# Splitting four weight pieces during the first slabs, loading the memory tokens later, and moving the softmax scaling ahead of the next scores in the third mixer

## Chip, cores and metric

The kernel runs on one core of a Trainium2 chip. The metric is the device time of one execution in microseconds (us), as the median over several runs; lower is better. The profile is of one execution, with its own time.

## The reference

There are 256 tokens of width 1024, in fp32. Two layers of a first block are followed by one layer of a second.

```
# first_block, for each of 2 layers
x = LN(alpha*x + 0.5*swiglu(x, gate[l,0], up[l,0], down[l,0]))      # first FFN
mem_kv = mem @ w_kv_mem[l]                                        # 256 memory tokens
u = x @ w_in
tok = short_conv_mixer(u) if l == 0 else mlstm_mixer(u)
xa = memory_cross_attention(u[..., -256:], mem_kv)
x = LN(alpha*x + concat(tok, xa) @ w_out[l])
x = LN(alpha*x + 0.5*swiglu(x, gate[l,1], up[l,1], down[l,1]))
# second_block
h = LN(x);  proj = h @ w_in
gates = sigmoid(g_logits + b_gate)                                # 3 branches of 1024
merged = gates[0]*y_pool + gates[1]*y_conv + gates[2]*y_mla       # "third mixer"
h = LN(alpha2*h + merged @ w_out)
h = LN(alpha2*h + moe(h) + ple(p, h))                             # top 2 of 16 experts
```

y_mla is attention of 8 heads with 96-wide queries and keys over two blocks of 128 queries: scores, a mask by chunks of 64, softmax, times the values. y_conv holds a causal depthwise convolution of 31 taps.

## The kernel before

**Arithmetic.** Each fp32 operand is split in a high part (a cast to fp32r) and a low part (the rest), and each product is three matmuls: high by high, low by high, high by low.

**The weight stream.** The weights of the first block and of the third mixer are one list of pieces of 128 x 1024. SyncE loads blocks of two pieces (the first blocks hold one or two) into three raw buffers (`load`, L284). `cast` (L297) writes the high part `wh` of a piece on ScalarE, and `low` (L305) the low part `wl` on VectorE; both go to one of 10 slots of a ring, whose numbers are in the names (`wh4`, `wl4`). A slot is free when `release` has been called for the piece that held it. `st.pump(n)` splits up to n further pieces at that place in the program if slots are free. The load of the block two ahead is issued when the first piece of a block is cast. Every engine works through its instructions in the order in which the program issues them.

**The start.** `first` calls `start_slabs`, which multiplies the pieces 0 to 3 (gate and up weights of the first 256 hidden columns) with the two token tiles, called slabs 0 and 1, while the input is still being transposed. `evacA(t, ps)` then takes the silu on ScalarE (`fs`, L435) and the product with the up part on VectorE (`fm`, L437). Next, `mem_load` issues three loads on ScalarE's queue: `par`, a table of small parameters, and the two tiles of `mem` (L715, L718). After it, `body` of the FFN runs: `slabT(t)` transposes a slab's hidden values on TensorE (L444) and splits them (`fhh` on ScalarE, L583); `gu(f, 0, T)` multiplies the gate and up pieces of hidden block f (pieces 4 and 5 for f=2, 6 and 7 for f=3); `both(f)` multiplies with the down pieces. `mem_T` transposes the memory tokens from f=3 on (L688).

**The third mixer.** `merge(0, ...)` multiplies gate pieces (`g`, `G`) and branch pieces (`y`) in the order of `MERGE_PLAN[0]`, and after each takes one step (one word) of the generator `mla()`, whose order is the string `MLA_PLAN` (L151). s, n, t and o stand for scores, norm, turn and out, and the digit for one of four chains (two blocks of queries by two halves of the heads). `scores` has matmuls (L1566) and then, for each of two groups of heads, a mask, a row maximum and its scaling on VectorE (L1571, L1573, L1574), and two exponentials on ScalarE (L1577). `norm` has a reciprocal on VectorE (L1584) and four scalings on ScalarE (L1587). `turn` transposes the probabilities on TensorE (L1599) and copies them on ScalarE; `out` multiplies with the values (L1613). Between them `merge` also pumps the stream and runs steps of the convolution: `tap` issues three taps on VectorE (L1654), `tap3` a group on TensorE (L1646) with diagonals that ScalarE writes (L1642). The gate's product `gb` is L1731.

Of the kernel before, what the change touches and what calls it, by code (L numbers as in the profile page):

```python
# [147 lines left out]
OFF_Q = 1536  # L148
OFF_GATE = 2208
MERGE = (0, 2, 1)  # L150
MLA_PLAN = "s0 s1+n0 - t0+n1 - o0+t1 - o1+s2 s3+n2 - t2+n3 - o2+t3 o3"  # L151
TAPS_BODY = "1110"
TAPS_POOL = "1011112312111112", "0000010111010111"
TAPS_MLA = "1111111010202032", "1111111010000000"
# [239 lines left out]
class FFN:  # L394
# [59 lines left out]
    def body(self):  # L454
        st = self.st
        self.acc = [[self.k.acc() for _ in range(2)] for _ in range(2)]

        def both(f):
            for t in range(2):
                self.down(f, t, t == 1)  # L460
            st.pump(2)

        self.slabT(0)
        st.pump(2)
        self.gu(2, 0, T)
        self.slabT(1)
        st.pump(2)
        for f in range(3, NF):
            self.gu(f, 0, T)
            st.pump(2)  # L470
            if f == 3:
                both(0)
                both(1)
            if f == 8:
                self.k.load_gb(self.nc.gpsimd if self.k.lnrow else self.nc.scalar)
            if f <= NF - self.last:
                both(f - 1)
            if self.li == (0, 0):
                if 0 < KV_AT[0] - f <= 2:
                    self.k.mem_T(f - KV_AT[0] + 2)  # L480
                if f in KV_AT:
                    self.k.memkv(*divmod(KV_AT.index(f), 3))
        for f in range(NF - self.last, NF):
            self.down(f, 0, False)
            st.pump(2)
        return self.acc
# [13 lines left out]
class Kernel:  # L500
# [17 lines left out]
    def mm(self):  # L518
        self.cmm = (self.cmm + 1) % self.nmm
        return self.slot(self.cmm)  # L520
# [65 lines left out]
    def mm3(self, out, lh, ll, rh, rl, first, last):  # L586
        mm = self.nc.tensor.matmul
        mm(out, lh, rh, start=first, stop=False)  # L588
        mm(out, lh, rl, start=False, stop=False)  # L589
        mm(out, ll, rh, start=False, stop=last)  # L590
# [599 lines left out]
    def start_slabs(self, f):  # L1190
        nc, st = self.nc, self.st
        mm = nc.tensor.matmul
        keys = [("gu", 0, 0, j) for j in range(4)]
        self.warmup = self.ringp.tile([P, P], F32, name=f"wh{RING - 1}")
        nc.vector.memset(self.warmup, 0.0)
        self.wps = self.mm()
        self.warm(8)
        tr = [self.transpose_steps(self.X[t], t, self.xh, self.xl) for t in range(2)]
        next(tr[0])
        self.warm(3)  # L1200
        ps = [self.mm() for _ in range(2)]
        hl = {}

        def part(t, js, x, late=False):
            s = slice(t * P, (t + 1) * P)
            for j in js:
                w = hl[j][x]
                for k in range(2):
                    kk = 2 * j + k
                    mm(ps[t], (self.xl if late else self.xh)[:, kk, s], w[:, k * 512:(k + 1) * 512],  # L1210
                       start=x + late + kk == 0, stop=x == 1 and kk == KT - 1)

        def get(j):
            st.cast()
            st.low()
            hl[j] = st.hl[j]

        get(0)
        get(1)
        part(0, (0, 1), 0)  # L1220
        for _ in tr[0]:
            pass
        part(0, (0, 1), 1)
        next(tr[1])
        get(2)
        get(3)
        for x in range(2):
            part(1, (0, 1), x)
        for _ in tr[1]:
            pass  # L1230
        part(0, (2,), 0)
        part(1, (2,), 0)
        part(0, (2,), 1)
        part(1, (2,), 1)
        part(0, (3,), 0)
        part(1, (3,), 0)
        part(0, range(4), 0, True)
        part(0, (3,), 1)
        f.evacA(0, ps[0])
        part(1, range(4), 0, True)  # L1240
        part(1, (3,), 1)
        for key in keys:
            st.release(key)
        f.evacA(1, ps[1])

    def first(self):
        fs, ws, fe = 0.5 / ALPHA, 1.0 / ALPHA, EPS / ALPHA ** 2
        f = FFN(self, 0, 0, "right")
        self.start_slabs(f)
        self.mem_load()  # L1250
        acc = f.body()
        self.slab_eng, self.slab_pumps, self.slab_ahead = self.nc.vector, 3, 2
        self.conv_open()
        self.ln_boundary(acc, fs, fe, f.tail, self.conv_head)
        acc = self.conv_body()
        g = FFN(self, 0, 1, "right")
        self.ln_boundary(acc, ws, fe, self.wout_tail, g.head)
        acc = g.body()
        f = FFN(self, 1, 0, "left")
        self.ln_boundary(acc, fs, fe, g.tail, f.head)  # L1260
        acc = f.body()
        self.ml_open()
        self.ln_boundary(acc, fs, fe, f.tail, self.ml_head)
        acc = self.ml_body()
        g = FFN(self, 1, 1, "right", LAST2)
        self.ln_boundary(acc, ws, fe, self.wout_tail, g.head)
        acc = g.body()
        return g, acc, fs, fe
# [280 lines left out]
    def mla(self):  # L1549
# [71 lines left out]

        for w in MLA_PLAN.split():
            if w != "-":
# [332 lines left out]
    def routing(self, p, mid):  # L1956
# [26 lines left out]

        gk = new("gk", 4)
        first(gs, misc[:, 148:152], 4, gk)
        ts(gk, gk, -1.0, 1e30, op0=OP.add, op1=OP.mult)
        sv = sel.rearrange("p t (g e) -> p t g e", g=4)
# [464 lines left out]
```

## Time and profile before

| | before |
|---|---|
| median of 3 runs | 1568.85 us (1566.15 to 1569.3) |
| profiled execution: its own time | 1567.56 us |
| profiled execution: span | 1565.6 us |
| mean granted TensorE clock | 0.989 |
| TensorE busy | 1515.4 us (97%) |
| VectorE busy | 881.5 us (56%) |
| ScalarE busy | 654.0 us (42%) |

The span is what the profiler records from the first instruction to the last, and the profiled execution's own time lies 1.96 us above it. A busy share is the time of an engine's own instructions over the span. The granted clock is a share of 2.4 GHz, so 0.50 is 1.2 GHz. PE is TensorE, DVE is VectorE, ACT is ScalarE, POOL is GpSimd, SP is SyncE.

### The profile page before, as it was taken

The page shows a single profiled execution, that of the slowest core. Times are in us where ns is not written, and L with a number is a line of the kernel's source. Part 1 is how long each engine was busy: PE and PEld are TensorE (multiplying, and loading weights), DVE is VectorE, ACT ScalarE, POOL GpSimd, SP SyncE. Part 2 cuts the span into 40 slices and gives each one's busy share as a digit, 9 for nine tenths or more (in the row PEclk, how much of TensorE's full clock was granted, in tenths as well). Part 3 has the DMA queues.
Part 4 walks back from the last instruction along what each step waited for, and adds up shares of the span by engine and source line. Part 5 has one row for each costly group of instructions (what it writes and reads, how often), then busy time and mean ns, then how long its engine had stood idle before and what let it go on. Part 6 is the DMA issues. An engine that isn't in the chain of part 4 may idle for free.

```text
span 1565.6 us, 23697 instructions
## 1 busy us (share of the span) xinstructions
PE 1515.4 (97%) x9725; PEld 1249.0 (80%) x9726; DVE 881.5 (56%) x1399; ACT 654.0 (42%) x1060; POOL 41.9 (3%) x63
## 2 busy tenths in 40 slices
PE   7999999999999999999999999989989999999996
PEld 6899998989999899998878999968879975434432
DVE  3565457775555755457867555578788565222223
ACT  3454445544444344445653444465654531111111
POOL 0000000000000000001001000020000000000001
PEclk9899999999999999999999999999999999999998
DMA  6465554445555454545334644535426666999991
GB/s 219 171 239 209 188 189 163 164 186 215 184 193 188 180 206 183 188 176 202 125 132 181 231 173 179 189 135 205 153 95 229 221 264 262 415 356 414 418 416 71
DMA packets 55985, 332.98 MB, mean 213 GB/s; under 512 B 6320, under 2 KB 6640, under 8 KB 24384
## 3 DMA queue, kind: packets, MB, share of 16 engines
q1 hardware_dynamic: 53424, 319.68, 54.0%
q0 software_dynamic: 1872, 9.52, 1.8%
q10 hardware_dynamic: 576, 2.22, 0.4%
q8 instruction: 78, 1.28, 0.3%
q14 instruction: 35, 0.29, 0.1%
HBM read 330.34 MB, written 1.05 MB: 212 GB/s over the span
## 4 chain that ended last, share of the span: by engine, by line
PE 81%; DVE 9%; ACT 5%; DMA 2%; issue 2%; POOL 0%; SPq 0%; ACTq 0%; DVEq 0%; POOLq 0%
PE mm L598 12%; PE mm L600 12%; PE mm L599 11%; PE mm L2119 7%; PE acc L589 6%; PE acc L588 6%; PE acc L590 6%; PE mm L2142 4%; DVE wl L305 3%; DMA raw<-in_ws_dram 2%; ACT wh L297 2%; PE acc L598 1%; PE acc L599 1%; PE acc L600 1%; PE mm L2088 1%
## 5 line engine op out<-in xcount | busy, mean ns | idle before, releaser
L305 DVE TENSOR_TENSOR wl<-raw,wh 128x1024 fp32r<-128x1024 f32 (+1 forms) x403 | 474.3, 1217 | 137.1 <-ACT wh L297 136.4
L598 PE MATMUL mm<-xh,wh 128*128 128x256 f32 x1608 | 456.8, 284 | 8.9 <-ACT wh L297 6.8
L297 ACT CAST wh<-raw 128x1024 fp32r<-128x1024 f32 (+1 forms) x404 | 403.0, 1044 | 138.4 <-PE acc L590 45.7
L600 PE MATMUL mm<-xh,wl 128*128 128x256 f32 x1608 | 453.6, 282 | 1.2 <-DVE wl L305 1.2
L599 PE MATMUL mm<-xl,wh 128*128 128x256 f32 x1608 | 453.7, 282 | 0.0
L598 PEld LDWEIGHTS mm<-xh,wh 128*128 128x128 f32 x1608 | 305.8, 190 | 14.9 <-ACT wh L297 7.3
L600 PEld LDWEIGHTS mm<-xh,wl 128*128 128x128 f32 x1608 | 305.8, 190 | 1.7 <-DVE wl L305 1.7
L599 PEld LDWEIGHTS mm<-xl,wh 128*128 128x128 f32 x1608 | 305.3, 190 | 2.1
L414 ACT ACTIVATE fs<-mm 128x256 f32<-128x256 f32 x80 | 30.7, 384 | 293.5 <-PE mm L600 293.3
L416 DVE TENSOR_TENSOR fm<-fs,mm 128x256 f32<-128x256 f32 x80 | 33.6, 421 | 211.7 <-ACT fs L414 211.7
L588 PE MATMUL acc<-wh,fhh 128*128 128x512 f32 x352 | 139.8, 397 | 2.4 <-ACT wh L297 2.4
L589 PE MATMUL acc<-wl,fhh 128*128 128x512 f32 x352 | 140.4, 399 | 0.8 <-DVE wl L305 0.8
L590 PE MATMUL acc<-wh,fhl 128*128 128x512 f32 x352 | 139.7, 397 | 0.0
L588 PEld LDWEIGHTS acc<-wh,fhh 128*128 128x128 f32 x352 | 67.0, 190 | 16.0 <-ACT wh L297 2.6
L590 PEld LDWEIGHTS acc<-wh,fhl 128*128 128x128 f32 x352 | 66.9, 190 | 15.7
L589 PEld LDWEIGHTS acc<-wl,fhh 128*128 128x128 f32 x352 | 66.8, 190 | 14.2 <-DVE wl L305 1.1
L584 DVE TENSOR_TENSOR fhl<-fm,fhh 128x256 fp32r<-128x256 f32 x80 | 34.0, 426 | 37.8 <-ACT fhh L583 37.8
L2123 ACT ACTIVATE es<-mm 128x256 f32<-128x256 f32 x16 | 6.1, 383 | 110.9 <-PE mm L2119 110.9
L583 ACT CAST fhh<-fm 128x256 fp32r<-128x256 f32 x80 | 32.5, 406 | 45.0 <-DVE fm L416 45.0
L651 POOL TENSOR_TENSOR rs_r<-rs_v,nhalf 128x1 f32<-128x1 f32 (+3 forms) x21 | 17.8, 847 | 1198.4 <-DVE rs_v L649 1154.1
L2157 DVE SCALAR_TENSOR_TENSOR X<-mm,ws,X 64x512 fp32r<-64x512 f32 x32 | 24.0, 750 | 37.3 <-ACT X L2154 36.7
L2124 DVE TENSOR_TENSOR es<-es,mm 128x256 f32<-128x256 f32 x16 | 6.7, 421 | 66.2 <-ACT es L2123 66.2
(609 smaller groups left out, 2127.2 us busy)
## 6 DMA issues: line engine op xcount, KB each, us to landing
raw<-in_ws_dram SPq DMA_DIRECT2D x196, 1024.0 KB, 4.9
wh<-in_we_dram SPq DMA_DIRECT2D x56, 512.0 KB, 11.2
wl<-in_we_dram SPq DMA_DIRECT2D x56, 512.0 KB, 11.2
w<-in_we_dram SPq DMA_DIRECT2D x22, 1024.0 KB, 11.3
raw<-in_we_dram SPq DMA_DIRECT2D x18, 1024.0 KB, 11.9
gb<-in_lnp_dram POOLq DMA_DIRECT2D x5, 1024.0 KB, 5.2
w<-in_wg_dram SPq DMA_DIRECT2D x2, 1024.0 KB, 7.7
raw<-in_ws_dram SPq DMA_DIRECT2D x2, 896.0 KB, 4.7
```

The costliest lines, as they stand in the source:

```text
L297: self.nc.scalar.copy(h[:, :n], src)
L305: self.eng.tensor_sub(l, src, h)
L416: nc.vector.tensor_tensor(m[:, :n], s[:, :n], ps[:, n:2 * n], op=OP.mult)
L584: self.nc.vector.tensor_sub(l, src, h)
L588: mm(out, lh, rh, start=first, stop=False)
L589: mm(out, lh, rl, start=False, stop=False)
L590: mm(out, ll, rh, start=False, stop=last)
L598: mm(out, h[:, c], xh[:, k, s], start=k == 0, stop=False)
L599: mm(out, h[:, c], xl[:, k, s], start=False, stop=False)
L600: mm(out, l[:, c], xh[:, k, s], start=False, stop=k == kn - 1)
L2119: nc.tensor.matmul(ps[64 * b:64 * b + 64], x, w[:, c:c + 512], start=d == 0, stop=d == KT - 1)
L2142: self.nc.tensor.matmul((pb if i else pa)[64 * i:64 * i + 64], hT[:, a, 64 * b:64 * b + 64], w[:, c:c + 512], start=k == 0, stop=k == 3)
```

## The change

Three edits. (1) `start_slabs` pumps two pieces when slab 1's input transposes have been issued, and one after each `evacA`: pieces 4 to 7 are split there, not in `body`. (2) `mem_load` is called in `body` of the first FFN, behind `slabT(1)` and the pump after it. (3) `MLA_PLAN` is another string of 14 words with the same 16 operations: each norm stands a word earlier against the scores behind it, and some words are empty.

```
--- before.py
+++ after.py
@@ -148,7 +148,7 @@
 OFF_Q = 1536
 OFF_GATE = 2208
 MERGE = (0, 2, 1)
-MLA_PLAN = "s0 s1+n0 - t0+n1 - o0+t1 - o1+s2 s3+n2 - t2+n3 - o2+t3 o3"
+MLA_PLAN = "s0 - n0+s1 - t0 n1 o0+t1 o1+s2 - n2+s3 - t2+n3 o2+t3 o3"
 TAPS_BODY = "1110"
 TAPS_POOL = "1011112312111112", "0000010111010111"
 TAPS_MLA = "1111111010202032", "1111111010000000"
@@ -465,6 +465,8 @@
         self.gu(2, 0, T)
         self.slabT(1)
         st.pump(2)
+        if self.li == (0, 0):
+            self.k.mem_load()
         for f in range(3, NF):
             self.gu(f, 0, T)
             st.pump(2)
@@ -1228,6 +1230,7 @@
             part(1, (0, 1), x)
         for _ in tr[1]:
             pass
+        st.pump(2)
         part(0, (2,), 0)
         part(1, (2,), 0)
         part(0, (2,), 1)
@@ -1237,17 +1240,18 @@
         part(0, range(4), 0, True)
         part(0, (3,), 1)
         f.evacA(0, ps[0])
+        st.pump(1)
         part(1, range(4), 0, True)
         part(1, (3,), 1)
         for key in keys:
             st.release(key)
         f.evacA(1, ps[1])
+        st.pump(1)
 
     def first(self):
         fs, ws, fe = 0.5 / ALPHA, 1.0 / ALPHA, EPS / ALPHA ** 2
         f = FFN(self, 0, 0, "right")
         self.start_slabs(f)
-        self.mem_load()
         acc = f.body()
         self.slab_eng, self.slab_pumps, self.slab_ahead = self.nc.vector, 3, 2
         self.conv_open()
```

ScalarE at the program's start, from the last cast of the first four pieces on (`raw` are the raw buffers, `mm` PSUM tiles). Before:

```order
L297 CAST wh3_166<-raw_80 128x1024
L435 ACT_TABLE_LOAD
L435 ACTIVATE fs_202<-mm2_126 128x256
L435 ACTIVATE fs_216<-mm3_127 128x256
L715 DMA par_71<-in_par_dram 128x230
L718 DMA mem0_224<-in_mem_dram 128x1024
L718 DMA mem1_225<-in_mem_dram 128x1024
L583 CAST fhh_235<-mm0_232 128x128
L583 CAST fhh_239<-mm0_232 128x128
L297 CAST wh4_245<-raw_132 128x1024
L297 CAST wh5_249<-raw_132 128x1024
L414 ACTIVATE fs_304<-mm1_253 128x256
```

And in the changed kernel, from the same cast on (line numbers of `body` are higher by two there):

```order
L297 CAST wh3_166<-raw_80 128x1024
L297 CAST wh4_182<-raw_132 128x1024
L297 CAST wh5_186<-raw_132 128x1024
L435 ACT_TABLE_LOAD
L435 ACTIVATE fs_212<-mm2_126 128x256
L297 CAST wh6_218<-raw_160 128x1024
L435 ACTIVATE fs_232<-mm3_127 128x256
L297 CAST wh7_236<-raw_160 128x1024
L585 CAST fhh_247<-mm0_244 128x128
L585 CAST fhh_251<-mm0_244 128x128
L297 CAST wh8_257<-raw_180 128x1024
L297 CAST wh9_261<-raw_180 128x1024
```

Two of the four casts now stand ahead of slab 0's silu and one behind each silu; the three loads are gone from here: six rows lie between the last row shown and them, the last two of which are the casts into slots 0 and 1.

VectorE in the third mixer around the first reciprocal (`sm`), from the last reduction of the first scores on. Before:

```order
L1574 TENSOR_SCALAR mx_11076<-mx_11076 128x2
L305 TENSOR_TENSOR wl2_11085<-raw_10937,wh2_11084 128x1024
L1654 SCALAR_TENSOR_TENSOR cz_10432<-cz_10432,par_71 128x256 x3
L1571 MEMSET acc_11116 64x2x64
L1573 TENSOR_REDUCE mx_11124<-acc_11116 128x2
L1574 TENSOR_SCALAR mx_11124<-mx_11124 128x2
L1571 MEMSET acc_11117 64x2x64
L1573 TENSOR_REDUCE mx_11131<-acc_11117 128x2
L1574 TENSOR_SCALAR mx_11131<-mx_11131 128x2
L1584 RECIPROCAL sm_11067<-sm_11067 128x4
L305 TENSOR_TENSOR wl3_11143<-raw_10937,wh3_11142 128x1024
```

And in the changed kernel, where lines of `mla` and `merge` are higher by four:

```order
L1578 TENSOR_SCALAR mx_11076<-mx_11076 128x2
L305 TENSOR_TENSOR wl2_11085<-raw_10937,wh2_11084 128x1024
L1658 SCALAR_TENSOR_TENSOR cz_10432<-cz_10432,par_71 128x256 x3
L305 TENSOR_TENSOR wl3_11117<-raw_10937,wh3_11116 128x1024
L1658 SCALAR_TENSOR_TENSOR cz_10432<-cz_10432,par_71 128x256 x6
L1735 SCALAR_TENSOR_TENSOR gb_10911<-sg_10076,acc_10912 128x256
L1588 RECIPROCAL sm_11067<-sm_11067 128x4
L1575 MEMSET acc_11145 64x2x64
L1577 TENSOR_REDUCE mx_11153<-acc_11145 128x2
L1578 TENSOR_SCALAR mx_11153<-mx_11153 128x2
```

The reciprocal now stands ahead of the second scores' reductions, but behind one more subtraction, six more taps and one gate product, as TensorE's second scores come one gate piece and one branch piece later.

## Rows read from the trace of the kernel before

**Rows 1.** The page's totals, and its chain that ended last, by engine.

```profile
PE 1515.4 (97%) x9725; PEld 1249.0 (80%) x9726; DVE 881.5 (56%) x1399; ACT 654.0 (42%) x1060; POOL 41.9 (3%) x63
...
PE 81%; DVE 9%; ACT 5%; DMA 2%; issue 2%; POOL 0%; SPq 0%; ACTq 0%; DVEq 0%; POOLq 0%
```

**Rows 2.** Windows: length; busy PE, PEld, DVE, ACT, POOL; clock; DMA share; GB/s.

```profile
160.00:560.00 400.00, 397.72 (x2705) 363.90 (x2705) 250.22 (x338) 182.68 (x276) 6.99 (x12) 1.00 0.51 187
560.00:1115.00 555.00, 546.08 (x3576) 487.56 (x3575) 351.07 (x525) 273.49 (x433) 21.35 (x24) 1.00 0.49 177
1320.00:1520.00 200.00, 200.00 (x967) 82.65 (x967) 47.04 (x98) 29.93 (x52) 2.70 (x6) 1.00 1.00 404
```

**Rows 3.** Timeline, TensorE's start: start, us, instruction, [idle before, releaser].

```profile
26.29 0.58 PE L598 MATMUL mm<-xh,wh 128*128 128x256 f32 x1 [3.72 <-ACT wh L297]
...
61.76 0.49 PE L688 MATMUL mm<-ident,mem 128*128 128x128 f32 x3
```

**Rows 4.** Windows of the start, columns as in the windows above.

```profile
22.19:61.76 39.57, 28.38 (x138) 24.59 (x137) 17.18 (x21) 14.38 (x21) 0.00 (x0) 0.78 0.45 164
26.30:32.60 6.30, 5.83 (x25) 5.54 (x26) 2.33 (x2) 0.88 (x1) 0.00 (x0) 0.50 0.66 247
40.20:43.10 2.90, 2.89 (x13) 2.90 (x14) 1.09 (x1) 0.00 (x0) 0.00 (x0) 0.51 0.27 42
49.90:56.70 6.80, 6.04 (x15) 4.66 (x15) 6.50 (x6) 4.38 (x6) 0.00 (x0) 0.50 0.52 196
```

**Rows 5.** Timeline of the start, ScalarE, its queue of DMA issues, and VectorE.

```profile
13.07 2.01 ACT L297 CAST wh<-raw 128x1024 fp32r<-128x1024 f32 x2
15.10 1.28 ACT L435 ACT_TABLE_LOAD   x1
16.45 1.28 DVE L695 TENSOR_TENSOR xl<-acc,xh 128x512 fp32r<-128x512 f32 x2
20.06 0.38 ACT L435 ACTIVATE fs<-mm 128x256 f32<-128x256 f32 x1 [3.68 <-PE mm L1210]
22.80 1.56 ACTq L718 DMA_DIRECT2D mem<-in_mem_dram  x2
25.19 1.99 ACT L297 CAST wh<-raw 128x1024 fp32r<-128x1024 f32 x2
```

**Rows 6.** The raw loads issued at 8 to 12 us: duration, starts, landing.

```profile
L284 SPq DMA_DIRECT2D raw<-in_ws_dram x2: 327/327/327, 9.2 to 10.9; - x2
...
DMA to landing us min/median/max: 7.4/7.7/8.1
```

**Rows 7.** Third mixer: TensorE's waits (sum, times, longest) in 1105 to 1190, and windows.

```profile
PE acc L1599 <- ACT pr L1587: 6.9, 3, 3.1
...
1120.00:1180.00 60.00, 51.23 (x360) 45.51 (x359) 45.51 (x106) 35.81 (x95) 3.18 (x6) 0.94 0.33 121
1130.00:1135.00 5.00, 2.55 (x18) 1.89 (x17) 1.91 (x7) 4.22 (x15) 0.00 (x0) 1.00 0.01 3
1140.00:1145.00 5.00, 4.08 (x11) 2.90 (x12) 3.91 (x9) 4.90 (x14) 0.00 (x0) 0.72 0.00 0
```

**Rows 8.** Timeline of the third mixer, VectorE and TensorE, in order of time.

```profile
1127.38 1.23 DVE L305 TENSOR_TENSOR wl<-raw,wh 128x1024 fp32r<-128x1024 f32 x1 [2.98 <-ACT wh L297]
1128.53 1.27 DVE L1654 SCALAR_TENSOR_TENSOR cz<-cz,par 128x256 f32<-128x256 f32 x3
1132.73 1.20 PE L1599 MATMUL acc<-ident,pr 128*128 128x128 f32 x4 [2.45 <-ACT pr L1587]
1135.66 2.46 DVE L1654 SCALAR_TENSOR_TENSOR cz<-cz,par 128x256 f32<-128x256 f32 x6
1138.04 0.41 DVE L1731 SCALAR_TENSOR_TENSOR gb<-sg,acc 128x256 f32<-128x256 f32 x1
1139.84 0.17 DVE L1584 RECIPROCAL sm<-sm 128x4 f32<-128x4 f32 x1
1140.56 1.21 PE L1599 MATMUL acc<-ident,pr 128*128 128x128 f32 x4 [3.15 <-ACT pr L1587]
```

More of the change, by code (lines that the diff above doesn't have):

```diff
@@ L150 @@
 MERGE = (0, 2, 1)
-MLA_PLAN = "s0 s1+n0 - t0+n1 - o0+t1 - o1+s2 s3+n2 - t2+n3 - o2+t3 o3"
+MLA_PLAN = "s0 - n0+s1 - t0 n1 o0+t1 o1+s2 - n2+s3 - t2+n3 o2+t3 o3"
 TAPS_BODY = "1110"
@@ L467, in body @@
         st.pump(2)
+        if self.li == (0, 0):
+            self.k.mem_load()
         for f in range(3, NF):
@@ L1230, in start_slabs @@
             pass
+        st.pump(2)
         part(0, (2,), 0)
@@ L1239, in start_slabs @@
         f.evacA(0, ps[0])
+        st.pump(1)
         part(1, range(4), 0, True)
@@ L1244, in start_slabs @@
         f.evacA(1, ps[1])
+        st.pump(1)
     def first(self):
@@ L1249, in first @@
         self.start_slabs(f)
-        self.mem_load()
         acc = f.body()
```

## The prediction

> **What bounds the kernel now.** I read the page's totals first: TensorE is busy for 97% of the span, and 81% of the chain that ended last is its own matmuls; VectorE has 9%, ScalarE 5% [rows 1]. So the question is where TensorE does not run, or runs at a lower clock. The windows of the long middle, 160 to 1115 us, have TensorE busy in 397.7 of 400 and 546.1 of 555 us at a granted clock of 1.00, and the window 1320 to 1520 in all of it [rows 2]. Little is to be had there. Two places remain.
>
> The first is the program's start. From the start of slab 0's transposes at 22.19 us to the memory transposes at 61.76 [rows 3] lie 39.57 us, of which TensorE is busy for 28.38 at a mean clock of 0.78 [rows 4]. It waits 3.72 us for the first cast of pieces 4 and 5 [rows 3], and three windows, each behind such a wait, run at a granted 0.50 or 0.51, the 1.2 GHz level: 6.30, 2.90 and 6.80 us [rows 4].
>
> The second is the third mixer's attention: in 1120 to 1180 TensorE stands for 60 − 51.23 = 8.77 us, and its clock is 0.94 [rows 7]. Of this idle time 6.9 us stands ahead of three `turn` transposes, which wait for ScalarE's scaling of the probabilities (largest 3.1) [rows 7]. VectorE is busy for 45.5 of those 60 us [rows 7], so it has only some 14 us to spare there.
>
> **The start, step by step.** No instruction is added or taken away; the splits of pieces 4 to 7 are moved ahead, and the loads of `par` and `mem` behind.
>
> - *Why pieces 4 to 7 are late now.* Their casts are issued behind slab 1's evacuation and behind the issues of the three loads of `mem_load`: ScalarE is issuing from 22.80 on (the two of `mem` alone 1.56 us), and its two casts begin at 25.19 [rows 5]. The raw block of pieces 4 and 5 had been loaded long before: issued at 9.2, 7.4 us to landing, so there at 16.6; that of 6 and 7 issued at 10.9, 8.1 us, so there at 19.0 [rows 6].
> - *Pieces 4 and 5 after.* ScalarE ends the casts of pieces 2 and 3 at 15.1 [rows 5] and waits for the block at 16.6; two casts of 2.01 us together [rows 5] take it to 18.6, and the table load of 1.28 [rows 5], which now stands behind them, to 19.9. Slab 0's silu starts at 20.06 now [rows 5], so it is not delayed, by 0.2 us. VectorE ends the two tiles of `xl` at about 17.7 [rows 5]; two subtractions of 1.23 [rows 8] end at 20.2, before slab 0's product needs it at 20.4. Both pieces are split some 2 us before TensorE wants them at 22.6.
> - *Pieces 6 and 7.* One cast behind slab 0's silu (20.4 to 21.5), one behind slab 1's (22.8 to 23.8); the last subtraction ends near 25.1. Step f=2 of the FFN keeps TensorE until about 28.2, so this is hidden with 3 us to spare.
> - *Later pieces.* Each raw buffer comes free when its subtractions end, so the loads of the next blocks go out about 6 to 9 us earlier than now, as the subtractions do; with 8.1 us each to landing [rows 6], pieces 8 and 9 are there by about 24.7 and wanted at 34, 10 and 11 by 28.2 and wanted at 40.
> - *The memory tokens.* Their issues now stand in ScalarE's queue behind the casts of pieces 10 and 11, by my walk at 33 to 35 us. With the landing time of the raw loads, 8.1 us, as a bound, they are there by 43.1; the transposes want them at about 42.7. That is nothing, or half a microsecond of waiting. The issues take about 2 us of ScalarE at 33 to 35, hidden by the matmuls of f=3. `par` has no reader before the first mixer.
> - *The sum.* In the three half-clock windows TensorE is busy for 5.83 + 2.89 + 6.04 = 14.76 us [rows 4]; at the full clock that is 7.38. The idle part of the whole stretch is 39.57 − 28.38 = 11.19. If no wait is left, the clock stays up and the gain is **18.6 us**. Some of the busy time that is left is pipeline overlap at a slow clock, so I take 19. Lower end 17: half a microsecond for the memory tokens and one short stretch at the lower clock. Upper end 20.
>
> What would stand late next? Nothing in the 1050 us behind: TensorE is the bound there [rows 2], loads go out when the pieces ahead of them are used, and so all of it moves with it. In the last stage TensorE is at 200 of 200 us and DMA at 1.00 [rows 2], but its loads too are issued when a tile comes free. The gain is kept.
>
> **The third mixer.** The first normalisation (`n0`: one reciprocal on VectorE, four scalings on ScalarE) now comes ahead of the second scores `s1`, and some `turn` and `out` steps come earlier. Again nothing is added.
>
> - *turn0.* Now the reciprocal stands behind the reductions of s1, and turn0 starts at 1132.73 after 2.45 us of waiting [rows 8]. In the new order the reciprocal has ahead of it wl2 (from 1127.38), three taps of the convolution, wl3, six taps and a gate: 1128.53 + 1.27 + 1.23 + 2.46 + 0.41 = 1133.9 [rows 8]. From a reciprocal at 1139.84 to its turn at 1140.56 it is 0.72 [rows 8], so turn0 starts at about **1134.6**, later than now. TensorE has in the meantime one more y (12 matmuls; 1.8 us at the 397.72/2705 = 0.147 of [rows 2], which holds wider ones) and one s1 without its wait: the 1.9 us of idle time not counted ahead of `turn` is mostly there. These two cancel, and it waits from about 1130.3 to 1134.6, some 4 us where it waits 2.45.
> - *turn1.* Its reciprocal comes after s1's exponentials (about 1136) and so with g4 and out0 as cover; the 3.15 us wait [rows 8] goes, or shrinks to 0.5.
> - *The clock.* The wait of 2.45 left it at 1.00 (1130 to 1135); behind that of 3.15 it is 0.72 in 1140 to 1145 [rows 7]: 0.28/0.5 of 5 us at half rate, 1.4 us lost. A wait of 4 us would cost between that and the 3.1 us lost behind the 3.72 us wait in the start (half of 6.30). I take 2.
> - *The Trainium skill* has a rule for this: in TensorE: Matmul & The Clock Gate, section "HAM oscillation — how this bites in real kernels", waits between short bursts of matmuls throttle TensorE again each time and the burst behind each runs cold. The trace agrees for 3.72 and 3.15 us and not for 2.45. By the rule applied to all waits the term would be about 1 us larger now and unchanged after; by the rows it stays as it is.
> - *Sum.* From s1 to s2 the same work lies in both orders. Now: 1.4 + 2.45 + 3.15 + 1.4 = 8.4 us lost. After: 4 + 2 + 0.5 = 6.5. That is 1.9 gained. The second half of the stage loses the rest, about 4 us (8.77 idle and 0.06/0.5 × 60/2 = 3.6 for the clock make 12.4 in all): turn2's wait may go, but its taps queue behind exponentials. I take −0.4 there, **1.5 us** gained together. Bounds: 3 lost (a turn0 wait with the full 3.1 us clock price and turn1 still waiting) and 6 gained (half of the 12.4).
>
> **Sum.** 19 + 1.5 = 20.5 us. The profiled execution took 1567.56, its span 1565.6; 1567.56 − 20.5 = 1547.1. The median of the runs, 1568.85, is 1.3 above it, so **1548.3 us**. A measurement of this kernel tells about 0.2% (3.1 us) from no change.
>
> **Rivals.**
> - *A. The third mixer gets back nearly all its waits* (10 of 12.4): 1568.85 − 19 − 10 = 1540. For it: the waits all hang on one small reciprocal. Against: VectorE's taps and subtractions now stand ahead of that reciprocal. 0.06.
> - *B. The third mixer loses 3 us:* 1568.85 − 19 + 3 = 1553. For it: turn0 is later by the sum above and the clock falls behind longer waits. 0.10.
> - *C. The stall only moves in the start:* pieces 8 to 11 or the memory tokens arrive late, a second wait keeps the clock at half rate, and about 9.5 of the 19 us come back: 1568.85 − 9.5 − 1.5 = 1558. For it: there are now two such later waits. Against: the landing times above leave 9 us or more. 0.06.
> - *D. Slower.* ScalarE works in order, and the casts of pieces 4 and 5 now stand ahead of slab 0's silu. Should their block land x later than 16.6, silu and all behind it move by x − 0.2. From x = 20.7 on, a load of 28 us where it is 7.4 now, the kernel is no faster: 1569 and, with 5 us more, 1574. Nothing in the rows does that. 0.02.
> - *E. No effect,* as the tail is limited by its transfers, which keep their times: 1568.85. Against: they are issued on demand. 0.01.
>
> Forecast 0.75, between 1544.5 and 1552. The range, 1543 to 1554.5, leaves out A, C, D and E, with 0.15 between them and a little of B. Faster by over 0.2%: 0.96; within: 0.02; slower: 0.02.
>
> **What would show it.** Right: no wait over 1 us ahead of the f=2 and f=3 matmuls, granted clock of 0.95 or more in 22 to 43 us, memory transposes near 42.6; turn0 waiting about 4 us, turn1 under 1. Wrong: a half-clock stretch that stays behind the slabs; a wait for `mem` ahead of its transposes; a wait that appears somewhere between 160 and 1520; turn0 starting less than 1 us after its matmuls are done, which would mean that VectorE's queue is shorter than I walked.

## The result, and the profile after

The changed kernel takes **1546.56 us** (median of 4 runs, 1545.39 to 1547.48), the kernel before beside it 1569.07; the ratio is 0.986, with a 95% interval of 0.9842 to 0.9877. That is 22.5 us less (19.3 to 24.8 by the interval), where 20.5 were forecast. The profiled execution has a span of 1544.8 us where it was 1565.6.

The page's totals after, against [rows 1]: the busy times of VectorE, ScalarE and GpSimd stay within 0.7 us. TensorE's falls by 8.5 us, with the same count of matmuls, and the other 12.3 of the 20.8 us of span are idle time.

```profile
PE 1506.9 (98%) x9725; PEld 1244.3 (81%) x9726; DVE 880.8 (57%) x1399; ACT 654.1 (42%) x1060; POOL 41.9 (3%) x63
```

**The start.** The window that answers to [rows 4], 22 to 43 us, and the timeline of ScalarE and its DMA queue that answers to [rows 5]. The casts at 15.83 are pieces 4 and 5, those at 20.11 and 22.44 pieces 6 and 7; the last row is TensorE's first transpose of the memory tokens.

```profile
22.00:43.00 21.00, 21.00 (x145) 19.30 (x144) 16.11 (x21) 13.36 (x20) 0.00 (x0) 1.00 0.78 302
```

```profile
15.83 2.00 ACT L297 CAST wh<-raw 128x1024 fp32r<-128x1024 f32 x2 [0.98 <-DMA raw<-in_ws_dram]
17.85 1.28 ACT L435 ACT_TABLE_LOAD   x1
19.83 0.39 ACT L435 ACTIVATE fs<-mm 128x256 f32<-128x256 f32 x1 [0.70 <-PE mm L1212]
20.11 1.04 ACT L297 CAST wh<-raw 128x1024 fp32r<-128x1024 f32 x1
22.44 1.04 ACT L297 CAST wh<-raw 128x1024 fp32r<-128x1024 f32 x1
...
30.12 0.37 ACTq L717 DMA_DIRECT2D par<-in_par_dram  x1
30.28 1.05 ACT L297 CAST wh<-raw 128x1024 fp32r<-128x1024 f32 x1
30.53 0.93 ACTq L720 DMA_DIRECT2D mem<-in_mem_dram  x2
...
42.23 1.04 PE L690 MATMUL mm<-ident,mem 128*128 128x128 f32 x8
```

TensorE is busy for 21.00 of 21.00 us at 1.00. The memory transposes start at 42.23 and not at 61.76 [rows 3]: 19.5 us earlier.

**The third mixer.** TensorE's steps that waited there, against [rows 7, 8]: the four transposes of turn0 (now two and two), turn1 (the four at 1126.81) and the groups of taps, L1603 and L1650 in this kernel; the scores s0 and s2 (L1570); and VectorE's queue ahead of the first reciprocal (L1588).

```profile
1102.80 1.15 PE L1570 MATMUL acc<-kf,qf 128*128 128x128 f32 x8
...
1116.44 0.77 PE L1603 MATMUL acc<-ident,pr 128*128 128x128 f32 x2 [4.00 <-ACT pr L1591]
...
1118.01 0.69 PE L1603 MATMUL acc<-ident,pr 128*128 128x128 f32 x2 [0.80 <-ACT pr L1581]
...
1126.81 0.66 PE L1603 MATMUL acc<-ident,pr 128*128 128x128 f32 x4
...
1130.80 1.99 PE L1570 MATMUL acc<-kf,qf 128*128 128x256 f32 x8
...
1147.83 1.99 PE L1650 MATMUL acc<-cz,tap 128*128 128x256 f32 x8 [1.85 <-ACT tap L1646]
...
1156.33 1.99 PE L1650 MATMUL acc<-cz,tap 128*128 128x256 f32 x8
```

```profile
1109.55 1.22 DVE L305 TENSOR_TENSOR wl<-raw,wh 128x1024 fp32r<-128x1024 f32 x1 [2.99 <-ACT wh L297]
1110.69 1.27 DVE L1658 SCALAR_TENSOR_TENSOR cz<-cz,par 128x256 f32<-128x256 f32 x3
1111.88 1.22 DVE L305 TENSOR_TENSOR wl<-raw,wh 128x1024 fp32r<-128x1024 f32 x1
1113.02 2.46 DVE L1658 SCALAR_TENSOR_TENSOR cz<-cz,par 128x256 f32<-128x256 f32 x6
1115.39 0.41 DVE L1735 SCALAR_TENSOR_TENSOR gb<-sg,acc 128x256 f32<-128x256 f32 x1
1115.72 0.17 DVE L1588 RECIPROCAL sm<-sm 128x4 f32<-128x4 f32 x1
```

turn0 waits for 4.00 us where it waited for 2.45, and turn1 for nothing where it waited for 3.15.

The starting points of the same work in the two traces show where the time came from. They are the first memory transpose, the first and third scores (s0, s2) and the last group of taps of the stage; those of before, where they are not among the rows ahead, come from this timeline of the kernel before:

```profile
1120.63 1.15 PE L1566 MATMUL acc<-kf,qf 128*128 128x128 f32 x8
...
1151.93 1.99 PE L1566 MATMUL acc<-kf,qf 128*128 128x256 f32 x8
...
1178.33 2.00 PE L1646 MATMUL acc<-cz,tap 128*128 128x256 f32 x8
```

| place | before, us | after, us | earlier by |
|---|---|---|---|
| memory transposes | 61.76 | 42.23 | 19.5 |
| s0 | 1120.63 | 1102.80 | 17.8 |
| s2 | 1151.93 | 1130.80 | 21.1 |
| last taps of the stage | 1178.33 | 1156.33 | 22.0 |
| end of the span | 1565.6 | 1544.8 | 20.8 |

The last column is called the lag below. In this pair of traces the start gave 19.5, 1.7 of it were gone by the third mixer, the third mixer gave 4.2 (3.3 up to s2, 0.9 behind it), and 1.2 went in the tail.

### The profile page after: what moved, and what is told of

It is laid out like the page before. It is cut to its first block, busy times and chain, and to the rows that moved or that the text cites. A ratio compares the mean times of both kernels' runs of the same rounds, so it can differ in the third digit from the quotient of the medians.

```text
span 1544.8 us, 23697 instructions
## 1 busy us (share of the span) xinstructions
PE 1506.9 (98%) x9725; PEld 1244.3 (81%) x9726; DVE 880.8 (57%) x1399; ACT 654.1 (42%) x1060; POOL 41.9 (3%) x63
## 4 chain that ended last, share of the span: by engine, by line
PE 82%; DVE 8%; ACT 5%; DMA 2%; issue 2%; POOL 0%; SPq 0%; ACTq 0%; DVEq 0%; POOLq 0%
PE mm L600 12%; PE mm L601 12%; PE mm L602 12%; PE mm L2123 7%; PE acc L590 6%; PE acc L591 6%; PE acc L592 6%; PE mm L2146 4%; DVE wl L305 3%; DMA raw<-in_ws_dram 2%; ACT wh L297 2%; PE acc L600 1%; PE acc L601 1%; PE acc L602 1%; PE mm L2092 1%
## 5 line engine op out<-in xcount | busy, mean ns | idle before, releaser
L653 POOL TENSOR_TENSOR rs_r<-rs_v,nhalf 128x1 f32<-128x1 f32 (+3 forms) x21 | 17.8, 847 | 1175.8 <-DVE rs_v L651 1131.5
```

## Experiments

Three theories stand against each other. Theory 1: start and plan are separate gains that add up, the start by the early splits, the plan through the place of one reciprocal in VectorE's queue. Theory 2: part of the start's gain is given back later, as the table suggests. Theory 3 is that another part of the change does the work (the later loads, or the plan in the start's wake). Times are medians; each ratio is to the kernel before, measured beside it.

### The start alone

```diff
 (the changed kernel, with)
-MLA_PLAN = "s0 - n0+s1 - t0 n1 o0+t1 o1+s2 - n2+s3 - t2+n3 o2+t3 o3"
+MLA_PLAN = "s0 s1+n0 - t0+n1 - o0+t1 - o1+s2 s3+n2 - t2+n3 - o2+t3 o3"
```

> Both edits of the start (three pumps, later mem_load) with the old MLA_PLAN. Theory 1 (start and plan add up, the start keeps what it gains): TensorE without a wait over 0.3 us from 22 to 43 us at a granted 1.00, memory transposes at 42.2 and not 61.8, total 19 to 19.6 us under the kernel before, about 1549.7. Theory 2 (part of the start's gain is given back in the middle, as the lag between the traces of before and after falls from 19.8 us at 700 us to 18 at 1100): the gain is 17 to 18, about 1551.5. Theory 3 (the gain hangs on the plan): less than 15.

1547.91 us against 1567.87, ratio 0.9872 (0.9857 to 0.9888): 20.0 us gained, between 17.6 and 22.4. The profile shows no wait of TensorE from 18 to 70 us; memory transposes at 41.95, 19.8 us earlier. That the gain hangs on the plan (theory 3) falls. The median is theory 1's, but the interval reaches down to the 17 to 18 of theory 2, and the span of the profiled execution is 18.2 us shorter; what tells the two apart comes below (the changed kernel once more).

The third mixer of this trace, in the old order, has rows that bear on the prediction's price of the clock: turn0, turn1 and the window behind turn0's wait.

```profile
1113.82 1.35 PE L1603 MATMUL acc<-ident,pr 128*128 128x128 f32 x4 [2.45 <-ACT pr L1591]
...
1121.64 1.21 PE L1603 MATMUL acc<-ident,pr 128*128 128x128 f32 x4 [0.77 <-ACT pr L1591]
```

```profile
1113.80:1119.80 6.00, 5.99 (x27) 5.66 (x28) 4.19 (x9) 3.99 (x9) 0.00 (x0) 0.50 0.30 93
```

The same wait of 2.45 us that left the clock at 1.00 in the kernel before [rows 7, 8] is followed by 0.50 here. It costs nothing: turn1 starts 7.82 us behind turn0, as in the kernel before (7.83), and waits 0.77 us where it waited 3.15. In the five traces with the old order turn1 comes 7.82 or 7.83 us behind turn0, whatever the clock did in between, and s0 to s2 takes 31.2 to 31.35 us. What sets turn1's start there is its reciprocal, which stands in VectorE's queue behind six taps and a gate product, among others [rows 8], and not TensorE.

### The plan alone

```diff
 (the kernel before)
-MLA_PLAN = "s0 s1+n0 - t0+n1 - o0+t1 - o1+s2 s3+n2 - t2+n3 - o2+t3 o3"
+MLA_PLAN = "s0 - n0+s1 - t0 n1 o0+t1 o1+s2 - n2+s3 - t2+n3 o2+t3 o3"
```

> Only the new MLA_PLAN. By the term of the prediction, 1.5 us gained (about 1567.5). By the lag of the two traces, which grows from 17.8 us ahead of the third mixer to 22.0 behind it, 4.2 us gained (about 1564.9). Rival: the longer wait ahead of turn0 (4.0 us) and the half clock behind it cost more than they give, 1 to 3 us slower. In the trace the wait ahead of turn0 should be 4.0 us in all three.

1565.40 us against 1567.87, ratio 0.9983 (0.9974 to 0.9992): 2.5 us gained, between 1.3 and 4.1. That interval holds the term of the prediction and ends just below the 4.2 that the lag grows by in the third mixer; a loss is ruled out. In its trace the stage, from s0 at 1123.29 to the last taps at 1176.93, takes 53.6 us where the kernel before takes 57.7 and the whole change 53.5: 4.1 less; but s0 itself is 2.7 us later there, of which more below (the changed kernel once more). The wait ahead of turn0 is 4.0 us and the later one for diagonals 1.85, as in the whole change. Start and plan add up to the 22.5 of the whole change within their intervals (that 20.0 + 2.5 hits it exactly is luck): theory 1, and nothing that can be told is left for theory 3's plan in the start's wake.

### The pumps without the later loads, and the later loads without the pumps

```diff
 (pumps only: the kernel before, in start_slabs)
         for _ in tr[1]:
             pass
+        st.pump(2)
...
         f.evacA(0, ps[0])
+        st.pump(1)
...
         f.evacA(1, ps[1])
+        st.pump(1)
```

> The three pumps alone, mem_load at its old place (so its three issues stand on ScalarE behind the cast of piece 7 and ahead of the slabs' splits), old MLA_PLAN. Theory 1 (the early casts are what counts): the same as with both edits of the start within 1 us, about 1550, no wait over 0.5 us in 22 to 43. Rival (the issues of the loads hold up ScalarE, or their 1 MB holds up the next raw blocks): a wait of 1 to 4 us returns at f=3 or ahead of the first down product, with half a clock behind it, 1554 to 1560.

1549.40 us against 1567.87, ratio 0.9882 (0.9867 to 0.9897), 18.5 us gained (16.1 to 20.9), and again no wait from 18 to 70 us; the memory transposes are at 41.94, as in the start alone at 41.95. The rival fell: up to there the loads cost nothing at their old place once the splits are early.

```diff
 (later loads only: the kernel before)
         self.start_slabs(f)
-        self.mem_load()
...
         self.slabT(1)
         st.pump(2)
+        if self.li == (0, 0):
+            self.k.mem_load()
```

> The later mem_load alone, no pumps, old MLA_PLAN. Theory 1: the casts of pieces 4 and 5 start about 2 us earlier, as the issues are gone from ahead of them; the first wait falls from 3.72 to under 2.5 us and with it the half-clock stretch of 6.3 us (3.1 lost); the waits at f=3 and ahead of the first down product stay; 4 to 6 us gained, about 1564. Rival (the issues were the cause of all the later waits): 15 us or more. Second rival: the wait only gets shorter by 2 us and the clock falls all the same, 2 us gained.

1567.07 us against 1567.87, ratio 0.9989 (0.9979 to 0.9998): 0.8 us gained, between 0.3 and 3.3. My expectation of 4 to 6 fell. Its timeline of TensorE, and the window of the first half-clock stretch:

```profile
24.60 0.58 PE L600 MATMUL mm<-xh,wh 128*128 128x256 f32 x1 [2.15 <-ACT wh L297]
...
25.86 0.58 PE L602 MATMUL mm<-xh,wl 128*128 128x256 f32 x1 [0.47 <-DVE wl L305]
...
60.26 1.04 PE L690 MATMUL mm<-ident,mem 128*128 128x128 f32 x8
```

```profile
24.60:31.40 6.80, 6.33 (x28) 6.04 (x29) 2.34 (x2) 0.90 (x1) 0.00 (x0) 0.50 0.45 154
```

The first wait falls to 2.15 us, as expected, but with 0.47 behind it the clock still falls to 0.50 for 6.8 us, and the later waits stay (3.12 and 2.37 us). The memory transposes are 1.5 us earlier, as the second rival had it.

### The first pump alone

```diff
 (the kernel before, in start_slabs)
         for _ in tr[1]:
             pass
+        st.pump(2)
```

> The kernel before with the first of the three pumps alone (pieces 4 and 5; no pump behind the evacuations, mem_load at its old place, old MLA_PLAN). Theory 1 (what counts is that the splits run two pieces ahead: every later pump then splits two pieces further on): ScalarE casts pieces 6 and 7 behind slab 0's transposes at about 25 to 27, TensorE wants them at 28; at most 0.5 us of waiting, and the gain of both edits of the start (20 us) within 1 us. Theory 2 (each of the three waits needs its own earlier split): the first wait of 3.72 and its half clock go, those at f=3 and ahead of the first down product stay, 7 to 10 us gained.

1549.86 us against 1566.32, 16.5 us less; ratio 0.9885 (0.9868 to 0.9902), that is 15.3 to 20.7. The median is not within 1 us of the 20 that theory 1 asked for, but far above the 7 to 10 of theory 2. The trace shows the start: no wait from 18 to 70 us, memory transposes at 42.19, 19.6 us earlier, where the whole start has 41.95. ScalarE's row for pieces 6 and 7 there, which stand behind the loads and slab 0's splits:

```profile
24.54 2.00 ACT L297 CAST wh<-raw 128x1024 fp32r<-128x1024 f32 x2
```

They are ready before TensorE comes to them at 28, as it does not wait there. Theory 1: each `pump(2)` in `body` takes the next two pieces, so one pump put ahead moves every later split two pieces on, and the three waits go together. The other two pumps and the later loads add 0.2 us up to the memory transposes; whether the 3.5 us between the two gains in time are more than the spread of the middle (below) stays open.

### The changed kernel once more

> The changed kernel once more, beside the kernels of this call. All theories: 22 to 23 us under the kernel before. Where the lag against the kernel before falls between 700 and 1100 us (1.5 us in its first trace): if that belongs to the change, it falls there again by as much; if it varies from one execution to the next, it may not.

1546.81 us against 1568.77, ratio 0.9861 (0.9846 to 0.9876). Its memory transposes are at 42.68 and its s0 at 1100.51: 19.1 and 20.1 us ahead of the kernel before. This time nothing is lost between them. The same stretches of the two executions of the same kernel, the first trace and this one:

```profile
880.00:980.00 100.00, 100.00 (x745) 95.31 (x745) 52.35 (x62) 44.30 (x63) 0.00 (x0) 1.00 0.50 182
...
1020.00:1040.00 20.00, 17.45 (x70) 13.22 (x69) 12.29 (x16) 15.12 (x29) 3.77 (x6) 0.91 0.54 169
```

```profile
880.00:980.00 100.00, 100.00 (x756) 95.56 (x755) 53.12 (x63) 44.87 (x63) 0.00 (x0) 1.00 0.50 180
...
1020.00:1040.00 20.00, 16.82 (x71) 12.04 (x70) 12.13 (x15) 14.02 (x28) 3.77 (x6) 1.00 0.66 214
```

In the first window all 100 us are busy at a granted 1.00 in both. Matched one by one, the 744 matmuls that the first execution starts there take 100.02 us in it and 99.14 in the second (some of the larger difference in the counts is that the two windows do not hold quite the same matmuls). The clock of 0.91 around 1030 is not what makes the difference: the matmuls of that window take 19.82 and 19.67 us. The thirteen traces kept settle whether the change loses time in the middle. From the memory transposes to s0 it takes 1058.9 to 1061.4 us in the three with the old start (mean 1060.5) and 1057.8 to 1063.4 in the ten with the new (mean 1060.6). The loss is thus not the change's; the kernel before happened to be the fastest of its three. Theory 2 falls for the middle.

The third mixer differs between the two executions too. The same wait for tap diagonals (1147.83 in the first) and the window behind it, in this one:

```profile
1145.52 2.77 PE L1650 MATMUL acc<-cz,tap 128*128 128x256 f32 x8 [1.85 <-ACT tap L1646]
```

```profile
1145.52:1150.00 4.48, 4.48 (x17) 4.00 (x18) 2.15 (x6) 4.01 (x10) 0.00 (x0) 0.62 0.00 0
```

With 1.85 us of waiting in both, the clock falls here and stays at 1.00 in the first trace, where the eight matmuls take 1.99.

### The place of six taps in VectorE's queue

```diff
 (the changed kernel; taps behind)
-TAPS_POOL = "1011112312111112", "0000010111010111"
+TAPS_POOL = "1211110312111112", "0000010111010111"
```

> The changed kernel with six convolution taps moved from ahead of the first reciprocal of the third mixer to behind the second scores' reductions (the digits of gate 3 and of branch 0 in TAPS_POOL: 2 and 0 become 0 and 2). Theory 1 (VectorE's queue ahead of the reciprocal is what makes turn0 wait): the reciprocal 2.46 us earlier, the wait ahead of turn0 4.0 to about 1.5, the half-clock stretch behind it shorter or gone, 2.5 to 4.5 us under the changed kernel. Rival (VectorE is the bound of this stage, so that the taps are paid wherever they stand): turn1's or a later wait grows by about 2.4, total within 1 us.

```diff
 (the changed kernel; taps ahead)
-TAPS_POOL = "1011112312111112", "0000010111010111"
+TAPS_POOL = "1011114112111112", "0000010111010111"
```

> The opposite: the changed kernel with six more taps ahead of the first reciprocal (4 and 1 in place of 2 and 3 for gate 3 and branch 3). Theory 1: the reciprocal and turn0 2.4 us later, a wait of 6.5, and 2.4 to 4 us more than the changed kernel. Rival: the taps taken away later give it back; within 1 us.

Taps behind: **1543.73 us**, 3.1 less than the changed kernel beside it, ratio 0.9845 (0.9831 to 0.9858). Taps ahead: 1549.63, 2.8 more, ratio 0.9875 (0.9860 to 0.9890). TensorE's waits from 1080 to 1170, and the window of the stage, with the taps behind:

```profile
PE acc L1650 <- ACT tap L1646: 1.8, 1, 1.8
PE acc L1603 <- ACT pr L1591: 1.6, 1, 1.6
PE acc L1650 <- issue: 1.4, 1, 1.4
```

```profile
1101.00:1156.00 55.00, 48.55 (x370) 44.22 (x370) 45.02 (x105) 35.29 (x96) 3.18 (x6) 1.00 0.34 122
```

And with the taps ahead the wait for turn0 and the window from then on:

```profile
1120.87 0.77 PE L1603 MATMUL acc<-ident,pr 128*128 128x128 f32 x2 [6.38 <-ACT pr L1591]
```

```profile
1116.90:1127.20 10.30, 5.53 (x20) 4.59 (x21) 8.09 (x23) 6.79 (x22) 0.00 (x0) 0.50 0.22 89
```

2.46 us of taps move the wait ahead of turn0 by 2.4 each way, 4.0 to 1.6 and to 6.4. Theory 1: the reciprocal's place is what turn0 waits for. The rival (taps are paid wherever they stand) fell. The kernel with the taps behind has the lowest median of those run; the next one cannot be told from it.

### Two further steps

```diff
 (the kernel with taps behind; a group of diagonals earlier)
-TAPS_POOL = "1211110312111112", "0000010111010111"
+TAPS_POOL = "1211110312111112", "0000010112000111"
```

> As the kernel with the taps behind, and one group of ScalarE's tap diagonals written at branch 4, ahead of the exponentials of the fourth chain, where it stood at branch 5 behind them (TAPS_POOL's second string). Theory 1: the wait of 1.85 us for these diagonals, late in the stage, goes and 1 to 2 us more are gained. Rival: the diagonals now hold up the exponentials by 1.3 us and turn2 waits for that: no gain.

1544.00 us, ratio 0.9840 (0.9826 to 0.9853). The wait of 1.85 us for the diagonals is gone, and `out` now waits 1.1 us for the copies of turn2's result, as ScalarE is late with those. No gain that can be told.

```diff
 (the kernel with taps behind; three more taps behind)
-TAPS_POOL = "1211110312111112", "0000010111010111"
+TAPS_POOL = "1212010312111112", "0000010111010111"
```

> As the kernel with the taps behind, and the three taps of gate 2 moved behind the second scores' reductions too (TAPS_POOL 1212010312111112), so that only two subtractions and a gate product stand ahead of the first reciprocal. Theory 1 (the reciprocal alone holds turn0): wait ahead of turn0 from 1.6 to 0.4 or less, 1 us less in all. Rival (ScalarE's chain of scalings, exponentials, a cast and gates comes next, as the wait for diagonals of 1.4 us behind turn0 suggests): that wait grows by as much, total within 0.5 us of the kernel with the taps behind.

1545.67 us against 1566.32, ratio 0.9859 (0.9842 to 0.9875). turn0 now waits 0.44 us, but the 1.4 us ahead of the taps behind it stays and turn1 waits 0.69. From s0, turn0 and the taps behind it start 1.2 us earlier than with the taps behind alone, but turn1 takes that back, as it now waits for ScalarE's scalings: s0 to s2 takes 25.55 us against 25.52. The rival is right that ScalarE's chain comes next and not in where: the wait that it named did not grow. The median is 1.9 us higher, in runs made at another time; in this trace 1.3 us go to the clock, which falls behind the late wait of 1.85 us for diagonals (the taps there take 3.27 us where they take 1.99). No gain.

### The first half of the plan

```diff
 (the changed kernel)
-MLA_PLAN = "s0 - n0+s1 - t0 n1 o0+t1 o1+s2 - n2+s3 - t2+n3 o2+t3 o3"
+MLA_PLAN = "s0 - n0+s1 - t0 n1 o0+t1 o1+s2 s3+n2 - t2+n3 - o2+t3 o3"
```

> The changed kernel with the last seven words of MLA_PLAN as they were before (s3+n2 - t2+n3 - o2+t3 o3 behind the new first seven). By the prediction the first half gives 1.9 and the second takes 0.4. By the traces (the lag grows from 17.8 at the first scores to 21.1 at the third scores and 22.0 behind the stage) the first half gives 3.3 and the second 0.9; then this kernel is 0.9 us slower than the changed one, with the 1.3 us wait ahead of turn2 and a half-clock stretch behind it back. Rival: the second half as it was costs nothing or is better, by up to 0.5.

1546.59 us against 1566.32, ratio 0.9872 (0.9855 to 0.9888): the time does not tell it from the changed kernel. In its trace, these starts:

```profile
1101.58 1.15 PE L1570 MATMUL acc<-kf,qf 128*128 128x128 f32 x8
...
1129.36 2.00 PE L1570 MATMUL acc<-kf,qf 128*128 128x256 f32 x8
...
1142.18 1.63 PE L1603 MATMUL acc<-ident,pr 128*128 128x128 f32 x8 [1.66 <-ACT pr L1591]
...
1156.10 2.00 PE L1650 MATMUL acc<-cz,tap 128*128 128x256 f32 x8
```

From s0 to s2 it takes 27.78 us where the kernel before takes 31.30: 3.5 gained; from s2 to the last taps 26.74 against 26.40: 0.3 lost. The wait ahead of turn2 is back, and the clock behind it falls to 0.50 (1144 to 1146). The changed kernel gains 0.9 there in the first trace; in the second, s2 is at 1128.48 and the last taps at 1154.97, which is 0.1 lost. So the first half gives the gain, 3.2 to 3.5 in the four traces that have it. The second half gives 0.9 where the clock stays up behind its wait of 1.85 us (the first trace, the plan alone) and nothing where it falls.

## Why the prediction was right

**The start: the mechanism and the size.** 19 us were forecast, 20.0 measured for the start alone (interval 17.6 to 22.4 from the ratio), 19.5 up to the memory transposes in the trace of after. The reason to be right is that the idle time and the half-clock time were both in the sum: 11.19 us of waits and 7.38 of clock. The steps held closely: casts of pieces 4 and 5 at 15.8 to 17.8 (16.6 to 18.6 forecast), silu of slab 0 at 19.83 and not delayed, pieces 6 and 7 in the two gaps behind the silus.

Two things in that part were wrong without harm. The loads of the memory tokens were expected at 33 to 35 us, behind the casts of pieces 10 and 11; they went out from 30.12 to 31.5, the first ahead of those casts (30.28) and the others while the first cast ran. And the prediction gave pumps and loads one sum, as if all were needed. The experiments with one part alone show that the first pump carries the gain and the later loads nothing.

**"The gain is kept": right for the middle, nearly for the tail.** Between the memory transposes and s0 the lag falls by 1.7 us in the first trace and grows by 1.0 in the second, with the same code, and over all traces it keeps its size. In the tail, from the last taps of the stage to the end of the span, some of it goes: 387.3 to 387.7 us in the three traces with the old start, 387.6 to 388.6 in the ten with the new, means 0.6 apart. In the first trace it is 1.2, of which 0.8 at one place, in the row below for the first transposes of the normed tokens. TensorE waited 0.19 us there before.

```profile
1259.26 0.66 PE L1768 MATMUL acc<-ident,X 128*128 128x128 f32 x4 [0.96 <-DVE X L677]
```

VectorE waits there for the scale and offset of the normalisation, a tile that is also called `gb`, whose load takes 7.7 us to land where it took 6.9. In the second trace of the changed kernel the wait is 1.24 us and in the start alone 0.59. Whether earlier weight loads crowd this one was not tried.

**The third mixer: the mechanism right, the size too small.** The queue ahead of the reciprocal came out as summed: from wl2's start to the reciprocal 1115.72 − 1109.55 = 6.17 us, where 1133.9 − 1127.38 = 6.5 were forecast. turn0 was to wait "some 4 us" and waits 4.00; turn1 was to wait 0.5 or less and does not wait. The wait costs clock: the window from 1114.9 to 1121.8 in the trace of after.

```profile
1114.90:1121.80 6.90, 4.55 (x18) 3.82 (x18) 4.69 (x14) 5.81 (x21) 0.00 (x0) 0.51 0.31 132
```

Half of 4.55 is 2.3 us, where 2 were taken. The rule on waits and the clock that the prediction quotes from the Trainium skill (TensorE: Matmul & The Clock Gate, section "HAM oscillation — how this bites in real kernels") agrees with this row and with the 6.38 us wait. The prediction's own ordering, by the length of a wait (2.45 left the clock up, 3.15 did not), held in its one trace by chance: behind 2.45 us the clock fell with the start alone, and behind waits of 1.32 and 1.66 ahead of turn2 it fell as well.

What was mis-sized is the time that the old order lost between s0 and s2: 8.4 was the term. Rows of the kernel before, the waits ahead of s1, the taps behind turn1 and the window of the clock there:

```profile
1125.78 0.49 PE L1566 MATMUL acc<-kf,qf 128*128 128x128 f32 x2 [1.18 <-ACT pr L1577]
1126.47 0.94 PE L1566 MATMUL acc<-kf,qf 128*128 128x128 f32 x6 [0.21 <-ACT pr L1577]
...
1142.13 3.65 PE L1646 MATMUL acc<-cz,tap 128*128 128x256 f32 x8 [0.37 <-issue]
```

```profile
1142.00:1146.00 4.00, 3.87 (x12) 3.19 (x13) 3.51 (x8) 3.00 (x9) 0.00 (x0) 0.57 0.00 0
```

The waits are 1.39 (ahead of s1), 2.45, 3.15 and 0.37, the last of which the term left out: 7.4 in all. The clock costs 0.43 of 4 us, 1.7, where the window 1140 to 1145 gave 1.4, as it ends within the slow stretch. And the slow issue behind the waits was not counted: turn0 and turn1 each took 1.20 and 1.21 us [rows 8] for four transposes that take 0.66 in the trace of after where nothing is waited for, as ScalarE delivers the probabilities one at a time, some 0.3 us apart (four scalings in 1.27 us from 1132.28 on). That is 1.1 us. Together 10.2 were lost, and 7.3 are left in the new order: waits of 4.00, 0.80 and 0.2 and 2.3 for the clock. The difference of 2.9 is near the 3.2 to 3.5 measured; the prediction had 1.9.

Nor are such terms independent, as the sum takes them: with the start alone the clock fell behind turn0 in the old order and turn1's wait shrank by 2.4 us, at no cost. The gain comes from turn1, ahead of which TensorE now has a group of taps and a gate piece to do (1121.26 to 1126.2 in the trace of after): the cover that the prediction named.

The second half was put at −0.4 and came out between −0.1 and 0.9. The kernel before loses there the wait ahead of turn2 and the clock behind it:

```profile
1164.40 1.63 PE L1599 MATMUL acc<-ident,pr 128*128 128x128 f32 x8 [1.32 <-ACT pr L1587]
```

```profile
1165.80:1169.30 3.50, 3.50 (x19) 3.50 (x18) 3.50 (x9) 2.88 (x7) 0.00 (x0) 0.54 0.00 0
```

In its place the changed kernel waits 1.85 us for diagonals ("its taps queue behind exponentials" in the forecast), with or without a fall of the clock. In time the plan's gain is 2.5 (1.3 to 4.1), so the 1.5 that was taken lies inside. That the whole came out near the forecast is in part luck: in the first pair of traces the start gave 0.5 us more than was taken and the plan 2.7 more, and the middle and the tail took 2.9 back.

**The rivals.** A (nearly all waits gone) did not come: 1.85 us of waiting for tap diagonals is new, and 4.00 for turn0 is longer. B and C did not come, as the rows above show. D needs a block landing late: the casts of pieces 4 and 5 wait for theirs and start at 15.83, where the landing was put at 16.6. E fell: the span ends 20.8 us earlier.

## What to carry to other kernels

Where a stream of prepared weights is taken on by relative steps ("split the next two"), count how many pieces it is ahead when the first matmuls come to them: one extra step at the first idle place of the preparing engines shifts all that follow, and the waits go together with the half-clock stretches behind them. When a short instruction is moved ahead in the program, list what is queued in front of it on its engine: here filler work placed ahead of one 0.17 us reciprocal cost TensorE as long as it lasted. Cost a wait as three parts: the idle time, the work behind it that trickles in as the late engine delivers, and the clock. Then look at the next wait behind it: if another engine sets when that one ends, it takes up the loss, and nothing is won by mending the first alone. And read the clock behind a wait from more than one execution before a price is put on it.

## What the runs showed of the hardware

- The length of a wait did not decide whether TensorE's clock fell behind it. In the start 2.15 us with 0.47 behind it left it at 0.50 for 6.8 us. In the third mixer the wait of 2.45 us ahead of turn0 left it at 1.00 in the kernel before [rows 7, 8] and was followed by 0.50 with the start alone. Behind the 1.85 us wait of the changed kernel it stayed at 1.00 in one execution and fell in the next, and so it went behind a wait of 1.60 us near 1030: 0.50 from 1030 to 1032 in the first (1020 to 1040: 0.91), 1.00 in the second. What decides is open.
- In one kernel, the same 744 matmuls took 100.02 us in one execution and 99.14 in another, both at a granted 1.00 with TensorE busy all the time. What sets this 0.9% is open.
- ScalarE's DMA issues of `par` and `mem` stand behind two casts in program order and went out ahead of them: `par` at 30.12, before the first of these began (30.28), and the two of `mem` by 31.00, before the second (31.23). The Trainium skill has it that a sequencer pushes engine instructions into a queue and goes on reading (Advanced Engine Details and Errata, section "Sequencer and Instruction Queues"); the trace agrees.
